# A hybrid layer on one core: the recurrence's output products of two blocks, moved from the end of the first phase into the projection of later blocks

## The chip, the cores and the metric

The kernel runs on one core of a Trainium2 chip. The metric is the device time of one execution in microseconds (us), here the median of three runs. The five engines are named as the profile names them: PE (TensorE, matrix products; PEld is its weight load), DVE (VectorE), ACT (ScalarE), POOL (GpSimd) and SP (SyncE, which here only issues DMAs). Each engine works through its own list of instructions in order. DMAs are issued from SP, ACT and POOL.

## The reference

One layer over a sequence of 2048 frames of width 1024, in float32. A projection feeds two mixers side by side: a delta-rule recurrence (RWKV-7, 8 heads of 64) and a differential attention (4 heads); their outputs share one output matrix, `w_out`. A cross attention to 256 memory tokens and a squared-ReLU MLP of width 4096 follow.

```
h = x
proj = rms_norm(h) @ w_in                       # 1792 columns recurrence, 1536 attention
y_rwkv = rwkv7_group(proj[:, :1792])            # sequential over frames, 512 wide
y_diff = diff_attn_group(proj[:, 1792:])        # block-causal, 512 wide
h = h + concat([y_rwkv, y_diff]) @ w_out
h = h + memory_cross_attn(rms_norm(h), rms_norm(mem))
h = h + square(relu(rms_norm(h) @ w_up)) @ w_down
out = rms_norm(h)
```

The rows 0 to 511 of `w_out` meet `y_rwkv`; the change is about this half of the product.

## The kernel before

Activations are held transposed, features on the 128 partitions and 512 frames (one of four blocks, numbered 0 to 3) on the free axis. Each large product is done in three matmuls per 128x128 weight tile, because both factors are split in a high and a low part (`whi`, `wlo` and, for activations, `xhi`/`xlo` or `yhi`/`ylo`): hi x hi, hi x lo, lo x hi. A weight half of 512 rows comes by one SP DMA of 256 KB into `wraw` (two buffers); ACT rounds it to `whi`, POOL subtracts for `wlo` (L612 to L616).

**The first phase** (`phase1`, L744) drives one stream of products, `inproj_stream` (L599), which yields after every three matmuls; three matmuls are a step. Its items are, in order: for each block the 26 column tiles of `w_in` (two lead tiles, 12 for the recurrence, 12 for the attention; 8 steps each), cut into eight segments; then seven attention tiles of block 3 held back (`late`); then the memory keys and values (`mem`, 16 items of 8 half-width steps), 8 products that fold `w_mo` into the values (`fold`), and the recurrence's output products (`wys`, 8 items of 4 steps for each of the four blocks). Of the latter, block 0's eight are interleaved with `mem` and `fold`; the 24 of blocks 1 to 3 come last (L840 to L844).

Around the stream runs the recurrence, in eight units (two per block, four heads each). `prep(u)` builds a unit's matrices and inverts them, `finish(u)` scans the 8 chunks and writes the result to a DRAM scratch, `s.yT` (L576). `run` (L911) sets how many stream steps are emitted between their pieces; both are wrapped in `urgent`, which gives their instructions a higher priority. The final order on each engine is written by the framework's planner, which takes priorities and a simulated timeline. The last two runs have `g.nd` = 170 steps beside `finish(6)` and `prep(7)`, and the rest beside `finish(7)` and `first_queries` (L941), the attention of block 0: four heads, two units each. Each such unit ends with L1136, which scales `ob`, and L1138, which stores it to `s.oT`.

An output product (`wy_items`, L711): before a block's first item, `pre` loads four slices of `s.yT` through `xsl` buffers (L723) and splits them into `yhi`/`ylo`, which take over the buffers of `xhi`/`xlo`. Each item loads the residual slice `xres` from `s.xT` on SP (L731) into a buffer of the tag `mix` (two buffers), runs 12 matmuls, adds on DVE (L738) and stores it back from ACT's queue (L739). The buffer is free when this store has landed.

`prep_x` (L232) fills `xhi`/`xlo` (one buffer each) at every block's start: eight slices, each a load into `xsl` (three buffers, L245), four transposes on PE (L247), a copy back into the same buffer on ACT (L249), a store to `s.xT` (L250), and the split. `x_stats` (L193) and `prep_mem` (L640) use the same three `xsl` buffers.

**The second phase** (`phase23`, L1471) first runs the rest of the layer for blocks 0 and 1 one after the other (`m_stream`, L1296), with the attention of blocks 1 to 3 (`d_stream`, L1142) interleaved, then blocks 2 and 3 together. `m_stream` for block 0 begins with `load_o` (L1287), which reads block 0's `s.oT` and splits it into `yh`/`yl` (L1221, L1222). The PSUM banks of the attention's scores in this phase are those that the first phase's `ps_acc` has used.

The 16 KiB per partition that the program builder sets aside for descriptors of POOL's DMAs is its default (L1544 gives no size). POOL issues in each unit a part of the transfers that carry the unit's matrices through DRAM (L418 to L468).

Of the kernel before, what the change touches and what calls it, by code (L numbers as in the profile page):

```python
# [16 lines left out]
P = 128  # L17
# [175 lines left out]
def x_stats(g, pool, blk):  # L193
    nc = g.nc
    ssx = g.small.tile([P, 2, 4], F32, tag="ssx", name="ssx")
    for j in range(4):
        for h in range(2):
            t = pool.tile([P, TB], F32, tag="xsl", name="xld", bufs=3)
            r0 = blk * TB + j * P
            nc.sync.dma_start(out=t, in_=g.i.x[0, r0:r0 + P, h * TB:(h + 1) * TB])  # L200
            nc.scalar.activation(out=t, in_=t, func=AF.Square, accum_out=ssx[:, h, j:j + 1])
    sst = g.small.tile([P, 4], F32, tag="sst", name="sst")
    nc.vector.tensor_tensor(out=sst, in0=ssx[:, 0, :], in1=ssx[:, 1, :], op=ALU.add)
    rstd = g.small.tile([P, 4], F32, tag="rstdx", name="rstdx")
    pow_rsqrt(g, rstd, sst, 4, 1.0 / D, RMS_EPS, "x")
    return rstd
# [25 lines left out]
def prep_x(g, pool, blk, rstd):  # L232
    nc = g.nc
    rows = slice(blk * TB, (blk + 1) * TB)
    psb = g.ps_acc.tile([P, TB], F32, tag="acc", name="psb")
    bcast_rows(g, psb, rstd, 4)
    sb = pool.tile([P, TB], F32, tag="sbx", name="sbx", bufs=1)
    nc.scalar.activation(out=sb, in_=psb, func=AF.Copy)
    out = []
    for k in range(KD):  # L240
        xt = pool.tile([P, 4, P], F32, tag="xsl", name="xsl", bufs=3)
        ps_pool, tag = (g.ps_misc, "misc") if blk == 0 and k % 2 else (g.ps_acc, "acc")
        ps = ps_pool.tile([P, TB], F32, tag=tag, name="ps_xt")
        if blk:
            nc.sync.dma_start(out=xt, in_=g.i.x[0, rows, k * P:(k + 1) * P].rearrange("(j p) c -> p j c", p=P))  # L245
        for j in range(4):
            nc.tensor.transpose(ps[:, j * P:(j + 1) * P], xt[:, j, :] if blk else g.xa[j][:, k * P:(k + 1) * P], g.ident)  # L247
        raw = xt.rearrange("p j c -> p (j c)")
        nc.scalar.activation(out=raw, in_=ps, func=AF.Copy)  # L249
        nc.sync.dma_start(out=g.s.xT[k * P:(k + 1) * P, rows], in_=raw)  # L250
        hi = pool.tile([P, TB], F32R, tag=f"xhi{k}", name="xhi", bufs=1)
        lo = pool.tile([P, TB], F32R, tag=f"xlo{k}", name="xlo", bufs=1)
        xn = pool.tile([P, TB], F32, tag="mix", name="xn", bufs=2)
        nc.vector.scalar_tensor_tensor(out=xn, in0=ps, scalar=g.col("nmix", k), in1=sb, op0=ALU.mult, op1=ALU.mult)
        nc.scalar.activation(out=hi, in_=xn, func=AF.Copy)
        eng = nc.gpsimd if blk == 0 and k % 2 else nc.vector
        eng.tensor_tensor(out=lo, in0=xn, in1=f32(hi), op=ALU.subtract)
        out.append((hi, lo))
    return out
# [380 lines left out]
def prep_mem(g, pool):  # L640
    nc = g.nc
    hs = [pool.tile([P, 2, MEMT], F32R, tag=f"xhi{k}", name="mh", bufs=1) for k in range(4)]
    ls = [pool.tile([P, 2, MEMT], F32R, tag=f"xlo{k}", name="ml", bufs=1) for k in range(4)]
    mh = lambda k: hs[k // 2][:, k % 2, :]
    ml = lambda k: ls[k // 2][:, k % 2, :]
    for j in range(2):
        ss = g.small.tile([P, 4], F32, tag="sst", name="ssm")
        ts_ = []
        for h in range(2):
            t = pool.tile([P, TB], F32, tag="xsl", name="mt", bufs=3)  # L650
            nc.sync.dma_start(out=t, in_=g.i.mem[0, j * P:(j + 1) * P, h * TB:(h + 1) * TB])
            junk = pool.tile([P, TB], F32, tag="mix", name="mj", bufs=2)
            nc.scalar.activation(out=junk, in_=t, func=AF.Square, accum_out=ss[:, h:h + 1])
            ts_.append(t)
        nc.vector.tensor_tensor(out=ss[:, 2:3], in0=ss[:, 0:1], in1=ss[:, 1:2], op=ALU.add)
        pow_rsqrt(g, ss[:, 3:4], ss[:, 2:3], 1, 1.0 / D, RMS_EPS, "x")
        for t in ts_:
            nc.vector.tensor_scalar(out=t, in0=t, scalar1=ss[:, 3:4], scalar2=None, op0=ALU.mult)
        ms = slice(j * P, (j + 1) * P)
        for k4 in range(2):  # L660
            ps = g.ps_acc.tile([P, 4, P], F32, tag="acc", name="ps_m")
            for k in range(4):
                nc.tensor.transpose(ps[:, k, :], ts_[k4][:, k * P:(k + 1) * P], g.ident)
            for k in range(4):
                kk = 4 * k4 + k
                w = g.col("nsrc", kk)
                nc.scalar.activation(out=mh(kk)[:, ms], in_=ps[:, k, :], func=AF.Copy, scale=w)
                nc.vector.scalar_tensor_tensor(out=ml(kk)[:, ms], in0=ps[:, k, :], scalar=w, in1=f32(mh(kk)[:, ms]),
                                               op0=ALU.mult, op1=ALU.subtract)
    return [(mh(k), ml(k)) for k in range(KD)]  # L670
# [37 lines left out]
    return kv, fold  # L708


def wy_items(g, pool, st, blk, key):  # L711
    nc = g.nc
    cs = slice(blk * TB, (blk + 1) * TB)
    xts = {}

    def pre(m):
        def f():
            if m == 0:
                ys = []
                for k in range(4):  # L720
                    kk = k + 4 * ((blk + 1) % 2)
                    raw = pool.tile([P, TB], F32, tag="xsl", name="yraw", bufs=3)
                    nc.sync.dma_start(out=raw, in_=g.s.yT[k * P:(k + 1) * P, cs])  # L723
                    hi = pool.tile([P, TB], F32R, tag=f"xhi{kk}", name="yhi", bufs=1)
                    lo = pool.tile([P, TB], F32R, tag=f"xlo{kk}", name="ylo", bufs=1)
                    nc.scalar.activation(out=hi, in_=raw, func=AF.Copy)
                    nc.vector.tensor_tensor(out=lo, in0=raw, in1=f32(hi), op=ALU.subtract)
                    ys.append((hi, lo))
                st[key] = [ys]
            xt = pool.tile([P, TB], F32, tag="mix", name="xres", bufs=2)  # L730
            nc.sync.dma_start(out=xt, in_=g.s.xT[m * P:(m + 1) * P, cs])  # L731
            xts[m] = xt
        return f

    def post(m):
        def f(ps):
            xt = xts[m]
            nc.vector.tensor_tensor(out=xt, in0=ps, in1=xt, op=ALU.add)  # L738
            nc.scalar.dma_start(out=g.s.xT[m * P:(m + 1) * P, cs], in_=xt)  # L739
        return f  # L740
    return [Item(key, g.i.w_out[0, :, m * P:(m + 1) * P], post(m), pre(m), TB, 1) for m in range(KD)]


def phase1(g, er):  # L744
# [3 lines left out]
    with ExitStack() as es:  # L748
# [81 lines left out]
        for b in range(1, NB):  # L830
            e = g.nlate if b == NB - 1 else 0
            segs.append(lead(b) + diffs(b, 0, 2) + rkv(2 * b) + diffs(b, 2, 3))
            a = min(2, 7 - e)
            segs.append(diffs(b, 5, a) + rkv(2 * b + 1) + diffs(b, 5 + a, 7 - e - a))
            if e:
                late = diffs(b, 12 - e, e)
        items = [it for sg in segs for it in sg] + late
        mem, fold = mem_items(g, pool, st, NB)
        wys = [it for b in range(NB) for it in wy_items(g, pool, st, b, NB + 1 + b)]
        for h in range(4):  # L840
            items += mem[2 * h:2 * h + 2] + wys[h:h + 1]
        for h in range(4):
# [68 lines left out]
        def run(gens, n):  # L911
            done = 0
            heads = [[next(x), i, x] for i, x in enumerate(gens)]
            while heads:
                h = min(heads)
                while done < h[0] * n:
                    next(stream, None)
                    done += 1
                t = next(h[2], None)
                if t is None:  # L920
                    heads.remove(h)
                else:
                    h[0] = t
            while done < n:
                next(stream, None)
                done += 1
        units = {}
        nst = [8 * len(sg) for sg in segs]
        rst[0] = x_first_stats(g, up)
        lora_load()  # L930
        run([], nst[0])
# [3 lines left out]
        run([urgent(g, finish(NU - 2), g.off_f), urgent(g, prep(NU - 1), g.off_p)], g.nd)  # L935
        el.close()
        dq = Ctx()
        run([urgent(g, finish(NU - 1, g.fin), g.off_f), urgent(g, first_queries(g, er, dq), g.off_q)], 8 * len(late) + 160 + 32 * NB - g.nd)


def first_queries(g, es, d):  # L941
# [15 lines left out]
def urgent(g, gen, offset):  # L957
    while True:
        with g.tc.high_priority(offset=offset):
            r = next(gen, None)  # L960
        if r is None and not isinstance(r, float) and gen.gi_frame is None:
            return
        yield r
# [592 lines left out]
```

## Time and profile before

| | |
|---|---|
| median of three runs | 3756.1 us (3751.57 to 3762.16) |
| profiled execution | 3768.81 us, its span 3767.1 us |
| PE busy | 3581.6 us, 95% of the span |
| DVE, ACT, POOL busy | 52%, 46%, 39% of the span |
| last projection matmul (L634) | starts at 1071.0 us |
| first use of `s.oT` by `m_stream` (L1221) | starts at 1422.1 us |

A busy PE counts the modelled length of a matmul from its start to its end, while the next one starts before that; so the distance from start to start tells what a matmul costs. Times are in us from the start of the span. The arrow in a row names what ended the idle time ahead of an instruction.

### The profile page before, as it was taken

To read this page: it belongs to the slowest core of one execution; us is meant where nothing else is said; L and a number is where in the kernel's file an instruction comes from. 1 tells how busy PE (TensorE), PEld (TensorE's weight loads), DVE (VectorE), ACT (ScalarE), POOL (GpSimd) and SP (SyncE) were. 2 spreads that over 40 slices of the span, in tenths; PEclk is the share of its full clock that TensorE was granted. 3 is DMA by queue.
4 is the path that set the end of the run, shared out by engine and by line. 5 is a ranking of instruction groups with operands and counts; after the bars stand their busy time and mean duration, and the time that the engine had idled before them with its cause. 6 is when DMAs were issued, how large, how long until landed. Compare 5 with 4: busy or idle time off the path is not lost. (4 is left out here: it accounts for less than half of the span.)

```text
span 3767.1 us, 57886 instructions
## 1 busy us (share of the span) xinstructions
PE 3581.6 (95%) x21297; PEld 2871.5 (76%) x21297; DVE 1957.9 (52%) x4093; ACT 1720.5 (46%) x3802; POOL 1464.5 (39%) x1195
## 2 busy tenths in 40 slices
PE   7999999999999878899999989999999999999998
PEld 5767766767777767678787777888878888888887
DVE  4456666666574636465566756666634332313132
ACT  5364464454455626554455765555543421212123
POOL 4424324423434534344435435343353332222225
PEclk9989999999999899999999999999999999999999
DMA  4343342333335674343324425232243331111113
GB/s 149 107 128 88 82 127 84 86 107 88 87 88 160 207 210 142 106 121 93 113 79 118 139 73 144 79 112 78 85 152 94 111 102 48 48 51 48 48 57 108
DMA packets 566066, 390.52 MB, mean 104 GB/s; under 512 B 65187, under 2 KB 491254, under 8 KB 565782
## 3 DMA queue, kind: packets, MB, share of 16 engines
q1 hardware_dynamic: 534134, 329.55, 30.5%
q10 hardware_dynamic: 28064, 50.35, 4.0%
q0 software_dynamic: 3584, 6.92, 0.8%
q8 instruction: 168, 2.75, 0.3%
q14 instruction: 116, 0.95, 0.1%
HBM read 311.14 MB, written 75.56 MB: 103 GB/s over the span
## 5 line engine op out<-in xcount | busy, mean ns | idle before, releaser
L170 POOL TENSOR_TENSOR wlo<-wraw,whi 128x512 fp32r<-128x512 f32 x520 | 689.5, 1327 | 1247.6 <-ACT whi L169 1218.6
L616 POOL TENSOR_TENSOR wlo<-wraw,whi 128x512 fp32r<-128x512 f32 x288 | 413.8, 1438 | 597.4 <-ACT whi L615 479.3
L169 ACT ACTIVATE whi<-wraw 128x512 fp32r<-128x512 f32 x520 | 327.9, 631 | 639.9 <-PE ps_dn L187 327.0
L186 PE MATMUL ps_dn<-hdh,whi 128*128 128x512 f32 x1024 | 402.1, 393 | 2.3 <-DVE t L1408 1.2
L187 PE MATMUL ps_dn<-hdl,whi 128*128 128x512 f32 x1024 | 401.8, 393 | 0.3 <-DVE hdl L1413 0.3
L188 PE MATMUL ps_dn<-hdh,wlo 128*128 128x512 f32 x1024 | 398.8, 393 | 3.3 <-POOL wlo L170 3.1
L186 PE MATMUL ps_up<-h2h,whi 128*128 128x512 f32 x1024 | 400.1, 391 | 1.0 <-DVE t L1408 0.9
L187 PE MATMUL ps_up<-h2l,whi 128*128 128x512 f32 x1024 | 400.7, 391 | 0.0
L188 PE MATMUL ps_up<-h2h,wlo 128*128 128x512 f32 x1024 | 395.3, 391 | 0.8 <-POOL wlo L170 0.8
L631 PE MATMUL ps_acc<-xhi,whi 128*128 128x512 f32 x832 | 343.7, 414 | 20.0 <-ACT carry L278 18.9
L634 PE MATMUL ps_acc<-xhi,wlo 128*128 128x512 f32 x832 | 343.8, 414 | 2.2 <-POOL wlo L616 2.0
L632 PE MATMUL ps_acc<-xlo,whi 128*128 128x512 f32 x832 | 340.3, 409 | 0.0
L615 ACT ACTIVATE whi<-wraw 128x512 fp32r<-128x512 f32 x288 | 181.2, 630 | 273.4 <-PE ps_acc L632 98.0
L1422 DVE TENSOR_TENSOR ht<-ht,ps_dn 128x512 f32<-128x512 f32 x128 | 87.8, 686 | 347.3 <-PE ps_dn L188 347.2
L1048 ACT ACTIVATE pt<-ps_s,nmx 128x512 f32<-128x512 f32 (+3 forms) x320 | 198.4, 621 | 142.4 <-DVE nmx L1047 117.9
L1047 DVE TENSOR_REDUCE nmx<-ps_s 128x1 f32<-128x512 f32 (+3 forms) x320 | 192.5, 606 | 75.6 <-PE ps_s L1044 71.6
L188 PEld LDWEIGHTS ps_dn<-hdh,wlo 128*128 128x128 f32 x1024 | 193.1, 189 | 45.3 <-POOL wlo L170 6.4
L186 PEld LDWEIGHTS ps_dn<-hdh,whi 128*128 128x128 f32 x1024 | 193.0, 188 | 41.8 <-issue 1.6
L186 PEld LDWEIGHTS ps_up<-h2h,whi 128*128 128x128 f32 x1024 | 192.1, 188 | 41.3 <-DVE t L1408 1.6
L187 PEld LDWEIGHTS ps_dn<-hdl,whi 128*128 128x128 f32 x1024 | 193.2, 189 | 39.8 <-DVE hdl L1413 0.5
L188 PEld LDWEIGHTS ps_up<-h2h,wlo 128*128 128x128 f32 x1024 | 192.4, 188 | 40.3 <-POOL wlo L170 1.5
L187 PEld LDWEIGHTS ps_up<-h2l,whi 128*128 128x128 f32 x1024 | 192.3, 188 | 38.8
(336 smaller groups left out, 7772.4 us busy)
## 6 DMA issues: line engine op xcount, KB each, us to landing
wraw<-in_w_in_dram SPq DMA_DIRECT2D x208, 256.0 KB
wraw<-in_w_down_dram SPq DMA_DIRECT2D x208, 256.0 KB
wraw<-in_w_up_dram SPq DMA_DIRECT2D x192, 256.0 KB
s_hT<-xt ACTq DMA_DIRECT2D x64, 256.0 KB
wraw<-in_w_out_dram SPq DMA_DIRECT2D x56, 256.0 KB
s_qkvT<-qkv ACTq DMA_DIRECT2D x48, 256.0 KB
wraw<-in_w_mq_dram SPq DMA_DIRECT2D x48, 256.0 KB
wraw<-s_mb SPq DMA_DIRECT2D x48, 256.0 KB
```

The costliest lines, as they stand in the source:

```text
L169: nc.scalar.activation(out=hi, in_=raw, func=AF.Copy)
L170: nc.gpsimd.tensor_tensor(out=lo, in0=raw, in1=f32(hi), op=ALU.subtract)
L186: nc.tensor.matmul(ps, whi(k), ahi(k), start=(k == 0), stop=False)
L187: nc.tensor.matmul(ps, whi(k), alo(k), start=False, stop=False)
L188: nc.tensor.matmul(ps, wlo(k), ahi(k), start=False, stop=(k == nk - 1))
L615: nc.scalar.activation(out=hi, in_=raw, func=AF.Copy)
L616: nc.gpsimd.tensor_tensor(out=lo, in0=raw, in1=f32(hi), op=ALU.subtract)
L631: nc.tensor.matmul(o, hi[:, kk, :], xs[k][0], start=(k == 0), stop=False)
L632: nc.tensor.matmul(o, hi[:, kk, :], xs[k][1], start=False, stop=False)
L634: nc.tensor.matmul(o, lo[:, kk, :], xs[k][0], start=False, stop=last)
L1047: nc.vector.tensor_reduce(out=nmx[:, m, c:c + 1], in_=ps[:, 0:w], axis=AX.X, op=ALU.max, negate=True)
L1048: nc.scalar.activation(out=pt[:, cw(c)], in_=ps[:, 0:w], func=AF.Exp, bias=nmx[:, m, c:c + 1], accum_out=sm[:, m, c:c + 1])
```

## The change

The eight output products of block 0 are put into the fifth and sixth segment (the projection of block 2), those of block 1 into the seventh and eighth (block 3). Each segment takes four, the first ahead of the segment's third last item, the others between the following items and after the last. They get tiles of their own, `yh0` to `yh3` and `yl0` to `yl3`, 16 KiB per partition. That space comes from `xsl`, which goes from three buffers to two in all its uses (2 KiB), and from the space for POOL's descriptors, which goes from the default to 2048 bytes (14 KiB). At the end of the phase block 2's eight products take the places that block 0's had, and block 3's eight come last. The count of steps follows: a segment's steps are now summed from its items, and the last run has 64 steps fewer.

```diff
-        xt = pool.tile([P, 4, P], F32, tag="xsl", name="xsl", bufs=3)
+        xt = pool.tile([P, 4, P], F32, tag="xsl", name="xsl", bufs=2)
...
-def wy_items(g, pool, st, blk, key):
+def wy_items(g, pool, st, blk, key, own=False):
...
-                    hi = pool.tile([P, TB], F32R, tag=f"xhi{kk}", name="yhi", bufs=1)
-                    lo = pool.tile([P, TB], F32R, tag=f"xlo{kk}", name="ylo", bufs=1)
+                    th, tl = (f"yh{k}", f"yl{k}") if own else (f"xhi{kk}", f"xlo{kk}")
+                    hi = pool.tile([P, TB], F32R, tag=th, name="yhi", bufs=1)
+                    lo = pool.tile([P, TB], F32R, tag=tl, name="ylo", bufs=1)
...
+        for b in range(NB - 2):
+            early = wy_items(g, pool, st, b, NB + 1 + b, True)
+            for j in range(2):
+                sg = segs[2 * b + 4 + j]
+                at = len(sg) - 3
+                for i, w in enumerate(early[4 * j:4 * j + 4]):
+                    sg.insert(min(at + 2 * i, len(sg)), w)
         items = [it for sg in segs for it in sg] + late
         mem, fold = mem_items(g, pool, st, NB)
-        wys = [it for b in range(NB) for it in wy_items(g, pool, st, b, NB + 1 + b)]
+        wys = [it for b in range(NB - 2, NB) for it in wy_items(g, pool, st, b, NB + 1 + b)]
...
-        nst = [8 * len(sg) for sg in segs]
+        nst = [sum(4 * it.nh for it in sg) for sg in segs]
...
-        run([urgent(g, finish(NU - 1, g.fin), g.off_f), urgent(g, first_queries(g, er, dq), g.off_q)], 8 * len(late) + 160 + 32 * NB - g.nd)
+        run([urgent(g, finish(NU - 1, g.fin), g.off_f), urgent(g, first_queries(g, er, dq), g.off_q)], 8 * len(late) + 160 + 64 - g.nd)
...
-    nc = _bacc.Bacc("TRN2", target_bir_lowering=False, num_devices=1)
+    nc = _bacc.Bacc("TRN2", target_bir_lowering=False, num_devices=1, dynamic_dma_scratch_size=2048)
```

The other lines of the diff set `bufs=2` for `xsl` in `x_stats`, `prep_mem` and `wy_items`.

## Rows read from the trace of the kernel before

**Rows 1.** Windows: stretch, length, busy PE, PEld, DVE, ACT, POOL, clock, DMA share, GB/s.
```profile
1312.00:1424.00 112.00, 86.89 (x367) 68.11 (x365) 37.56 (x87) 30.72 (x67) 37.30 (x31) 0.92 0.70 203
...
300.00:1071.00 771.00, 742.05 (x6413) 542.50 (x6412) 485.40 (x1225) 376.77 (x917) 283.34 (x251) 0.96 0.34 94
```

**Rows 2.** Waits of all engines, 1240 to 1430: total us, times, longest.
```profile
DVE xres L738 <- DMA xres<-s_xT: 45.9, 16, 6.4
PE ps_acc L631 <- DVE xres L738: 19.1, 11, 4.2
```

**Rows 3.** Waits of SP's queue, 1240 to 1430.
```profile
SPq L731 <- DMA s_xT<-xres: 56.0, 17, 6.5
```

**Rows 4.** Timeline of PE, end of the projection: start, us, instruction.
```profile
1069.16 0.40 PE L631 MATMUL ps_acc<-xhi,whi 128*128 128x512 f32 x1
...
1071.00 0.39 PE L634 MATMUL ps_acc<-xhi,wlo 128*128 128x512 f32 x1
```

**Rows 5.** Waits of PE, 300 to 1070.
```profile
PE ps_acc L631 <- ACT carry L278: 13.8, 9, 2.1
...
PE ps_xt L247 <- DMA xsl<-in_x_dram: 3.2, 1, 3.2
```

**Rows 6.** Waits of PE, 1071 to 1240.
```profile
PE ps_acc L631 <- DVE xres L738: 1.3, 1, 1.3
```

**Rows 7.** Timeline of DVE, first and last addition of the trailing 24 products.
```profile
1319.87 0.69 DVE L738 TENSOR_TENSOR xres<-ps_acc,xres 128x512 f32<-128x512 f32 x1 [5.71 <-DMA xres<-s_xT]
...
1418.36 0.69 DVE L738 TENSOR_TENSOR xres<-ps_acc,xres 128x512 f32<-128x512 f32 x1 [2.11 <-DMA xres<-s_xT]
```

**Rows 8.** Timeline of DVE, ends of three units of the first phase's attention.
```profile
1290.41 0.40 DVE L1136 SCALAR_TENSOR_TENSOR ob<-ob,d_sub,psb 128x256 f32<-128x256 f32 x1
...
1310.87 0.47 DVE L1136 SCALAR_TENSOR_TENSOR ob<-ob,d_sub,psb 128x256 f32<-128x256 f32 x1
...
1397.44 0.47 DVE L1136 SCALAR_TENSOR_TENSOR ob<-ob,d_sub,psb 128x256 f32<-128x256 f32 x1
```

**Rows 9.** Timeline of PE and ACT where the second phase begins.
```profile
1419.11 0.80 PE L1043 MATMUL ps_s<-ks,qa 128*128 128x512 f32 x1 [3.64 <-DVE xres L738]
...
1421.09 0.69 ACT L1048 ACTIVATE pt<-ps_s,nmx 128x512 f32<-128x512 f32 x1 [17.41 <-DMA s_xT<-xres]
...
1422.12 1.14 ACT L1221 ACTIVATE yh<-yraw 128x512 fp32r<-128x512 f32 x2
```

**Rows 10.** Line 985, 1200 to 1423: count, ns min/median/max, first and last start.
```profile
L985 ACT ACTIVATE ks<-draw x10: 615/632/634, 1225.2 to 1312.5; 128x512 fp32r<-128x512 f32 x10
```

**Rows 11.** Timelines of PE, SP and DVE while block 3's slices are prepared.
```profile
796.35 0.66 PE L247 MATMUL ps_xt<-ident,xsl 128*128 128x128 f32 x4
...
798.40 0.34 SPq L250 DMA_DIRECT2D s_xT<-xsl  x1
...
802.21 0.37 SPq L245 DMA_DIRECT2D xsl<-in_x_dram  x1
...
819.23 0.38 SPq L245 DMA_DIRECT2D xsl<-in_x_dram  x1
...
824.21 0.66 PE L247 MATMUL ps_xt<-ident,xsl 128*128 128x128 f32 x4 [3.22 <-DMA xsl<-in_x_dram]
...
829.32 0.68 DVE L257 TENSOR_TENSOR xlo<-xn,xhi 128x512 fp32r<-128x512 f32 x1
```

**Rows 12.** Windows of 10 us while block 1's slices are prepared.
```profile
220.00:230.00 10.00, 7.24 (x55) 4.70 (x55) 9.71 (x20) 5.87 (x15) 2.58 (x1) 0.89 0.44 142
230.00:240.00 10.00, 10.00 (x61) 8.18 (x61) 9.78 (x18) 7.02 (x18) 0.00 (x0) 0.50 0.42 131
240.00:250.00 10.00, 10.00 (x58) 7.97 (x58) 9.06 (x17) 5.25 (x14) 0.70 (x1) 0.50 0.50 156
```

**Rows 13.** POOL's DMA issues of one kind, whole run (count, busy, mean ns, idle before).
```profile
L468 POOL DMA_DIRECT2D NTs<-LT x16 | 9.3, 588 | 8.0 <-DMA LT<-X 8.0
```

**Rows 14.** Waits of POOL, 700 to 1180.
```profile
POOL NTs L468 <- DMA LT<-X: 5.0, 3, 3.3
```

More of the change, by code (lines that the diff above doesn't have):

```diff
@@ L197, in x_stats @@
         for h in range(2):
-            t = pool.tile([P, TB], F32, tag="xsl", name="xld", bufs=3)
+            t = pool.tile([P, TB], F32, tag="xsl", name="xld", bufs=2)
             r0 = blk * TB + j * P
@@ L649, in prep_mem @@
         for h in range(2):
-            t = pool.tile([P, TB], F32, tag="xsl", name="mt", bufs=3)
+            t = pool.tile([P, TB], F32, tag="xsl", name="mt", bufs=2)
             nc.sync.dma_start(out=t, in_=g.i.mem[0, j * P:(j + 1) * P, h * TB:(h + 1) * TB])
@@ L721, in f @@
                     kk = k + 4 * ((blk + 1) % 2)
-                    raw = pool.tile([P, TB], F32, tag="xsl", name="yraw", bufs=3)
+                    raw = pool.tile([P, TB], F32, tag="xsl", name="yraw", bufs=2)
                     nc.sync.dma_start(out=raw, in_=g.s.yT[k * P:(k + 1) * P, cs])
-                    hi = pool.tile([P, TB], F32R, tag=f"xhi{kk}", name="yhi", bufs=1)
-                    lo = pool.tile([P, TB], F32R, tag=f"xlo{kk}", name="ylo", bufs=1)
+                    th, tl = (f"yh{k}", f"yl{k}") if own else (f"xhi{kk}", f"xlo{kk}")
+                    hi = pool.tile([P, TB], F32R, tag=th, name="yhi", bufs=1)
+                    lo = pool.tile([P, TB], F32R, tag=tl, name="ylo", bufs=1)
                     nc.scalar.activation(out=hi, in_=raw, func=AF.Copy)
```

## The prediction

> **What bounds the kernel now.** I read the windows first, to see where PE has room. Over the projection, 300 to 1071 us, PE is busy 742 of 771 us; over the end of the first phase, 1312 to 1424, it is busy 86.9 of 112, with the DMA engines at a share of 0.70 against 0.34 in the projection [rows 1]. So the projection is PE's own, and the end is not: 25.1 us of it are idle.
>
> The waits say who holds the end. DVE's addition of the residual (L738) waits 45.9 us for the load of `xres`, and PE waits 19.1 us for that addition, because the product cannot start before one of its two PSUM buffers is free [rows 2]. SP's queue in turn waits 56.0 us, before it may issue the load of `xres`, for the landing of an earlier store of the same buffer [rows 3]. That is a loop of load, add, store over two `mix` buffers, and each product has to go through it. When such products lie between items of another kind (block 0's eight, 1100 to 1240), the same wait of PE is 1.3 us [rows 6]. The loop only binds when products follow each other.
>
> **What a product costs in each place.** Two matmuls of the projection start 1069.16 and 1071.00, eight intervals apart: 0.23 us each [rows 4]. A product of 12 costs PE 12 x 0.23 = 2.76 us where PE is the bound. In the trailing run of 24, the first addition starts at 1319.87 and the last at 1418.36: 98.5 / 23 = 4.28 us a product [rows 7].
>
> **The change, part by part**, against the profiled execution (3768.8 us, 12.7 above the median; I carry the difference over to the median).
>
> 1. Sixteen products into the projection. PE is the bound there: + 16 x 2.76 = + 44.2 us. With each product come a weight load, a conversion on ACT, a subtraction on POOL, one residual load and one store; these engines and the DMAs have the room of [rows 1] (POOL 283 of 771 us, ACT 377). Each product lies between projection items of 24 matmuls, 5.5 us, in which its buffer's store can land; [rows 6] is the nearest row for that, so I take no wait. If the cover failed, each would cost the 4.28 of the end: 16 x 1.52 = 24 us more.
> 2. Idle time that they fill. PE waits 13.8 us in the projection for an item's last copy on ACT (L278), with both PSUM buffers held [rows 5]. A product between two such items gives the copy 2.76 us more. Only some of the sixteen stand there (in the eighth segment, beside recurrence tiles): between 0 and 13.8, and I take - 4.
> 3. Two `xsl` buffers instead of three. From block 3's preparation I take one buffer's round: load 824.21 - 819.23 = 5.0, transposes 0.66, the copy on ACT about as long, and the store's landing 802.21 - 798.40 = 3.8; some 10.1 us [rows 11]. Over two buffers that is 5.05 us a slice, 40 us for eight; over three it took 829.32 + 0.68 - 796.35 = 33.7. So each of three boundaries gets some 7 us longer. PE has the recurrence to do meanwhile: with three buffers it waited 3.2 us for such a load in all of 300 to 1070 [rows 5]. Bounds 0 and 3 x 7 = 21 us; I take the lower part, + 6, since the row nearest shows PE nearly covered. A gain is excluded: nothing starts earlier for a buffer less.
> 4. Less space for POOL's descriptors. The rows show its issues short (0.59 us for the smaller gather [rows 13]) and waiting only for data. No row shows an issue that waits for space. I take 0; the other end is rival D.
> 5. Sixteen products out of the trailing run: - 16 x 4.28 = - 68.5 us, if nothing else becomes late.
> 6. What is late next: the attention of block 0 (`first_queries`). Its fifth unit ends at 1310.87, its eighth at 1397.44; those three had to queue behind DVE's and PE's waits for residuals, at 28.9 us each, while the fifth came 20.5 us after the fourth [rows 8]. `m_stream` needs the last one: its first conversion starts at 1422.12, and 17.4 of these 24.7 us ACT was held by a residual store [rows 9]. Without the trailing products I put the three units at 20.5 each and the handover at 24.7 - 17.4 = 7.3: 68.8 us after 1310.87 instead of 111.3, so `m_stream` starts 42.4 us earlier, not 68.5. In the gap of 26.1 us PE has two chains: `first_queries`, and the attention of blocks 1 to 3, whose first scores started at 1419.11 as soon as the last residual was added and PSUM came free [rows 9]; ten key conversions had been done by 1312.5, of which four are already its own, since the three later heads of block 0 need six [rows 10]. The three units took 86.9 - 24 x 2.76 = 20.7 us of PE [rows 1], in 61.5 us a share of 0.34; two chains 0.68. So 0.32 x 26.1 = + 8.4 us stay idle (bounds 0 and 26.1).
>
> Sum: + 44.2 - 4 + 6 + 0 - 68.5 + 8.4 = - 13.9 us, 3768.8 to 3754.9 on the profiled scale, **3742 us** on the scale of the median.
>
> **The rivals.**
>
> A, the forecast, has bounds of its own: without items 3 and the gap - 28.3 (3728), with a gap half idle and 9 us at the boundaries - 6 (3750).
>
> B: block 0's attention sets the end and nothing fills the gap. Then the end gives back 42.4, not 60: 44.2 - 4 + 6 - 42.4 = + 3.8, 3760; with 21 us at the boundaries 3775. For it: a unit is a chain over four engines that less PE work shortens little, and `m_stream` cannot start without it. Against it: the scores that were ready at 1419.
>
> C, slower: the two-buffer staging starves PE at the block boundaries. Its place is the three runs of `prep_x`. [...] Against it: at the boundaries of blocks 2 and 3 the wait was 3.2 us in all [rows 5], and at the last one a product that needs no `xhi` now closes the segment before.
>
> D: POOL's issues wait for descriptor space. If the four gathers that close an inverse went out one landing at a time, at the longest wait for a landing seen on POOL, 3.3 us [rows 14], a unit would come 3 x 3.3 = 10 us later. In the projection PE has other work; two units at the end have less: + 20, 3762; with all eight exposed + 80, 3822.
> [...] No run here shows at what size an issue would wait.
>
> That the products are not run where they are put is unlikely: they hold a place in one stream whose items share PSUM in turn.
>
> **How the numbers follow.** A 0.52, B 0.27, C 0.13, D 0.08. The measurement can tell about 0.3%, 11 us, from no change. Faster than 3745: most of A (0.40) and a little of B (0.03), 0.43. Within 11 us: the rest of A (0.12), most of B (0.22), some of D (0.03), 0.37. Slower: C, some of D and of B, 0.20. The range goes from 3716 (A's lower end, and 12 us in which the planner, with the end of the phase cleared, starts the second phase's attention still earlier) to 3774 (B with the boundaries at their bound); C and the far part of D lie outside. A alone: 3728 to 3750.
>
> **What would show it.** After the change, the last projection matmul (1071.0 [rows 4]) should start some 46 us later, near 1117; the distance between matmuls there stays 0.23. PE's wait for residual additions at the end of the phase should fall from 19.1 to under 8 us. The last `ob` should come within 65 us of the fifth, and the first `yh` conversion within 12 us of the last `ob`; scores of block 1 should start before it. If instead the projection's end moves by 60 us or more, with waits for `xsl` loads or clock slices at 0.50 at the boundaries, it was C; if POOL sits idle ahead of its DMA issues, D; if PE idles more than 15 us between the last product and the first `yh`, B. The forecast is wrong in its root if the sixteen products cost the 4.28 us in their new place too.

## The result and the profile after

The changed kernel takes 3781.2 us (median of four runs, 3778.3 to 3785.7) against 3753.9 (four runs of the kernel before beside it): a ratio of 1.0063, interval 1.0047 to 1.0080. By the ratio it is 24 us slower; 14 us faster was forecast. Its profiled execution took 3781.1 us, span 3779.4. In the sessions of the experiments, on four chips, the kernel before took 3762.8 to 3767.2 us (medians of 17 to 28 runs), and the changed kernel was not run there; so the size of the loss is less certain than its interval says.

What did come as forecast first. The DVE timeline of the kernel after (start, duration, the instruction) answers to [rows 7, 8]: the additions of the trailing run and two units of block 0's attention, the fifth and the last.

```profile
1383.16 0.47 DVE L1144 SCALAR_TENSOR_TENSOR ob<-ob,d_sub,psb 128x256 f32<-128x256 f32 x1
...
1409.21 0.69 DVE L739 TENSOR_TENSOR xres<-ps_acc,xres 128x512 f32<-128x512 f32 x1 [3.56 <-DMA xres<-s_xT]
...
1436.86 0.69 DVE L739 TENSOR_TENSOR xres<-ps_acc,xres 128x512 f32<-128x512 f32 x1 [4.13 <-DMA xres<-s_xT]
1440.85 0.48 DVE L1144 SCALAR_TENSOR_TENSOR ob<-ob,d_sub,psb 128x256 f32<-128x256 f32 x1 [0.71 <-PE psb L158]
```

The trailing run has eight products, at (1436.86 - 1409.21) / 7 = 3.95 us. From the fifth `ob` to the last it is 57.7 us (86.6 before), and the handover is short, as the first conversion of `m_stream` on ACT's timeline shows, 5.4 us after the last `ob` (24.7 before [rows 8, 9]):

```profile
1446.22 0.63 ACT L1229 ACTIVATE yh<-yraw 128x512 fp32r<-128x512 f32 x1 [0.48 <-issue]
```

PE's waits from 1240 to 1450 (total, times, longest) show that residual additions hold PE for the 3.4 us of this row and 0.5 us elsewhere, against 19.1 us [rows 2];

```profile
PE ps_s L1051 <- DVE xres L739: 3.4, 1, 3.4
```

and SP's queue waits for the stores of `xres` in the same stretch no longer than this, against 56.0 us [rows 3]:

```profile
SPq L732 <- DMA s_xT<-xres: 16.3, 4, 6.5
```

So the end of the phase is what was forecast in kind. But `m_stream` starts at 1446.2 instead of 1422.1, 24 us later. (The two profiled executions differ by only 12.3 us in the end, spans 3779.4 and 3767.1, because the second phase took 2333 us against 2345. That the 24 us here equal the 24 by the ratio is therefore partly luck.) The projection is still PE's, busy 835 of 873 us, as the window to its end shows (length, then PE busy), against 742 of 771 in [rows 1]:

```profile
300.00:1173.00 873.00, 835.39 (x6968) 609.40 (x6967) 540.61 (x1348) 409.62 (x995) 313.11 (x277) 0.96 0.36 102
```

Its last matmul, on PE's timeline, comes 102 us later than in [rows 4], not 46, at the same distance of 0.23 us:

```profile
1172.99 0.40 PE L632 MATMUL ps_acc<-xlo,whi 128*128 128x512 f32 x1
1173.22 0.40 PE L634 MATMUL ps_acc<-xhi,wlo 128*128 128x512 f32 x1
```

**Where the time went.** I split the first phase where the recurrence's last matrices are done (the last `A<-psw` of unit 7: 1183 before, 1250 after); from there on the last scan, block 0's attention and the rest of the stream run to the first `yh`. The windows (length, then PE busy and its instructions, PEld, DVE, ACT, POOL, granted clock) of the kernel before:

```profile
0.00:1183.00 1183.00, 1115.01 (x9199) 824.58 (x9200) 706.27 (x1776) 577.01 (x1381) 448.17 (x419) 0.95 0.37 104
1183.00:1422.00 239.00, 202.53 (x1176) 161.99 (x1175) 111.41 (x290) 116.29 (x278) 104.18 (x83) 0.92 0.67 199
```

and of the kernel after:

```profile
0.00:1250.00 1250.00, 1159.98 (x9327) 852.35 (x9327) 724.29 (x1799) 585.19 (x1396) 454.37 (x427) 0.94 0.37 107
1250.00:1446.00 196.00, 167.29 (x1062) 134.89 (x1058) 103.84 (x272) 107.04 (x270) 94.86 (x76) 0.93 0.60 180
```

PE issues the same work in both (10375 and 10389 matmuls to `yh`) and is busy 92 to 93% of the phase, so a product moved inside it can win little but idle time. The front grew by 67 us, the end shrank by 43. In the front PE's idle time (length less busy) rose from 68.0 to 90.0 us; in the end it fell only from 36.5 to 28.7. Idle time is thus 14 of the 24 us; for the other 10 PE was busy longer with nearly the same matmuls.

**The block boundaries.** The windows of the three units in which a block's slices are prepared (units 1, 3 and 5 of 0 to 7), before:

```profile
208.00:348.00 140.00, 136.18 (x1140) 99.52 (x1139) 93.67 (x236) 76.32 (x188) 49.42 (x43) 0.90 0.39 113
488.00:624.00 136.00, 129.51 (x1125) 94.75 (x1125) 94.94 (x232) 74.30 (x183) 48.94 (x42) 0.92 0.41 117
765.00:902.00 137.00, 129.58 (x1150) 96.40 (x1150) 94.28 (x230) 70.47 (x170) 46.73 (x43) 0.96 0.38 106
```

and after, with unit 4 (141 us before) between the last two:

```profile
211.00:360.00 149.00, 140.71 (x1135) 100.23 (x1134) 95.30 (x235) 76.17 (x189) 46.78 (x42) 0.89 0.37 107
496.00:650.00 154.00, 143.41 (x1150) 105.37 (x1148) 97.11 (x238) 79.52 (x193) 49.66 (x45) 0.90 0.41 116
650.00:800.00 150.00, 146.75 (x1184) 106.19 (x1180) 85.87 (x217) 64.92 (x158) 55.88 (x48) 0.97 0.32 91
800.00:958.00 158.00, 148.20 (x1215) 110.09 (x1212) 101.66 (x240) 76.55 (x181) 53.30 (x47) 0.91 0.43 122
```

The three take 9, 18 and 21 us longer: 48 of the front's 67 (some of it work: units 3 and 5 hold more matmuls, 25 and 65). But not all of this belongs to the buffer. In `after_x3` (below), which has three `xsl` buffers again, units 1, 3, 4 and 5 are:

```profile
207.00:355.00 148.00, 142.69 (x1141) 104.84 (x1141) 93.64 (x236) 76.73 (x190) 49.52 (x44) 0.86 0.39 109
488.00:628.00 140.00, 131.81 (x1138) 96.83 (x1138) 99.37 (x238) 78.73 (x192) 47.93 (x44) 0.94 0.45 125
628.00:765.00 137.00, 135.20 (x1158) 97.33 (x1157) 84.67 (x217) 63.66 (x157) 53.25 (x47) 0.99 0.34 94
765.00:928.00 163.00, 147.15 (x1210) 107.94 (x1209) 100.13 (x238) 77.96 (x181) 51.95 (x49) 0.95 0.43 120
```

The third buffer gives back 14 us in unit 3 and 13 in unit 4, and nothing in units 1 and 5. Unit 5 goes with the moved products: it takes 158 to 166 us in every kernel below with block 0's products early and three buffers, and 135 to 140 in those without. Unit 1 takes 148 us in `alias_only` too, which moves no product and has three buffers.

In ten-microsecond slices of unit 3, the kernel after, the granted clock is at the lower of its two levels for a whole slice and part of the next, after a slice in which PE was busy 8.64 of 10 us:

```profile
520.00:530.00 10.00, 8.64 (x80) 6.92 (x79) 9.77 (x17) 7.22 (x20) 1.33 (x1) 0.89 0.59 157
530.00:540.00 10.00, 9.35 (x56) 6.13 (x54) 6.63 (x13) 4.14 (x12) 1.25 (x2) 0.50 0.47 134
540.00:550.00 10.00, 10.00 (x81) 6.12 (x81) 5.61 (x11) 6.45 (x17) 1.78 (x3) 0.76 0.27 87
```

The kernel before has such a slice in this unit as well, so the clock does not tell the two apart here (for block 1 see [rows 12]):

```profile
520.00:530.00 10.00, 10.00 (x65) 6.75 (x63) 8.19 (x16) 5.65 (x16) 1.26 (x2) 0.59 0.56 160
```

PE's own waits from 300 to 1173, which answer to [rows 5] (13.8 and 3.2), name the slices for only 6.9 us (5.4 in `after_x3`):

```profile
PE ps_acc L631 <- ACT carry L278: 11.8, 10, 2.2
PE ps_xt L247 <- DMA xsl<-in_x_dram: 6.9, 6, 2.2
```

### The profile page after: what moved, and what is told of

It reads as the page before. It is cut to its first block, busy times and chain, and to the rows that moved or that the text cites. A ratio compares the mean times of both kernels' runs of the same rounds, so it can differ in the third digit from the quotient of the medians.

```text
span 3779.4 us, 57866 instructions
## 1 busy us (share of the span) xinstructions
PE 3589.3 (95%) x21297; PEld 2870.4 (76%) x21297; DVE 1969.6 (52%) x4093; ACT 1716.5 (45%) x3802; POOL 1459.9 (39%) x1195
```

## The experiments

Two executions with the same instruction order on every engine (the kernel before and `scratch_only`, below) differ by 21.6 us, and by 20 us already at the first `yh`. The ends of their fronts lie 18 us apart, 1183 and 1165, with PE idle for 68.0 and 62.5 us in them. So verdicts go by the ratios of many runs, one hundredth of which is 38 us; a single marker of a trace is good to some 20 us. The sessions ran on different chips, so a comparison of two ratios from different sessions also rests on the kernel before behaving alike on both. Also, the planner writes a new order for every edit; I take it, without a run that shows it, that kernels can differ by some 10 us for this alone.

**x2_only.** The kernel before with `xsl` alone cut:

```diff
-tag="xsl", ..., bufs=3
+tag="xsl", ..., bufs=2
```

> Before, with two xsl buffers instead of three and nothing else. Staging theory (the shorter buffer chain at the three block boundaries is the loss): 10 to 30 us slower than before, with the units that hold a boundary (about 208 to 348, 488 to 624, 765 to 902 us) each 5 to 15 us longer and the others unchanged. Displacement theory (the sixteen products cost the projection more than their 44 us of PE, or the end gives back too little): within 5 us of before. Descriptor theory (POOL waits for space): within 5 us of before.

Measured: 1.0030 (1.0013 to 1.0047), + 11 us (5 to 18). PE's idle time in the front rises from 68.0 to 80.8:

```profile
0.00:1195.00 1195.00, 1114.17 (x9199) 817.66 (x9200) 712.89 (x1776) 578.20 (x1382) 446.48 (x419) 0.95 0.36 103
```

The two buffers alone cost 11 us without a product moved; the 6 that I took lies just inside the interval. The sign that was to go with it came at one boundary of three: units 1, 3 and 5 take 149, 134 and 137 us.

**scratch_only.** The kernel before with the smaller descriptor space:

```diff
-num_devices=1)
+num_devices=1, dynamic_dma_scratch_size=2048)
```

> Before, with 2048 bytes for POOL's descriptors and nothing else; every engine's instructions stay in the same order. Descriptor theory: 10 us slower or more, with longer idle time ahead of or inside POOL's DMA issues (the smaller gather took 0.59 us). Staging and displacement theory: within 4 us of before.

Measured: 0.9992 (0.9980 to 1.0003). Rival D falls.

**after_x3.** The change with three `xsl` buffers; the room comes from writing the inverse's `T` into the buffer of `N`:

```diff
-tag="xsl", ..., bufs=2
+tag="xsl", ..., bufs=3
-        u.T = lp.tile([P, NCK, CH], F32, tag="T", name="T", bufs=2)
+        u.T = TT[:, p]        # TT = lp.tile([P, 2, NCK, CH], F32, tag="N", ...)
```

> After, with three xsl buffers again; the 2 KiB come from the inverse's pool, where the merged matrices T take over the buffer of N, which is dead by then. Staging theory: the boundary units fall back by some 10 us each, 20 to 40 us faster than after, so 0 to 15 us faster than before. Displacement theory: like after, some 25 us slower than before.

Measured: 0.9997 (0.9982 to 1.0013): the loss is gone, and so is any gain. Against the change itself, 1.0063, the third buffer is worth 0.66%, 25 us (16 to 34). The two ratios come from different sessions; the plain medians, 3781.2 and 3771.1, are 10 us apart. The front ends at 1220 instead of 1250:

```profile
0.00:1220.00 1220.00, 1141.11 (x9283) 841.90 (x9283) 720.73 (x1798) 583.04 (x1389) 448.02 (x425) 0.95 0.39 109
1220.00:1425.00 205.00, 172.62 (x1096) 139.60 (x1094) 100.15 (x271) 107.52 (x272) 96.47 (x78) 0.91 0.61 180
```

**alias_only**, its control: the kernel before with that `T` in `N` and the small descriptor space.

> A control: the kernel before with the smaller descriptor space and the transform T written into the buffer of N, as in after_x3 and the kernels made from it; no product is moved and xsl keeps three buffers. If that edit is harmless, as the comparisons with after_x3, only0 and only1 assume, the ratio is 0.998 to 1.002, the projection ends within 6 us of 1071 and block 0's last inverse within 8 us of 1183. If the edit itself delays or speeds a unit (T can be written only when N's last readers are done, and the next N only when T's are), the ends of the units drift from 208, 348, 488, 624, 765, 902, 1044, 1183 by a constant amount per unit, and the ratio leaves 0.998 to 1.002; the gain of only0 (0.9923) is then partly the alias.

Measured: 1.0012 (0.9998 to 1.0025), inside the bound for harmless; in its trace, whose time was 10 us above its median, unit 7 ended at 1194, past the 8 us allowed. If the sharing costs anything, it is some 5 us (9 at most by the interval), and it makes the kernels that carry it look worse, not better.

**only0** and **only1.** after_x3 with the eight products of only one block early:

```diff
-        for b in range(NB - 2):
+        for b in [0]:        # only1: [1]
```

> As after with three xsl buffers, but only block 0's eight products are early (fifth and sixth segment); block 1's go back to the end of the phase. Alignment theory (the early products of block 0 push block 3's slice preparation, at 796 to 830 us before, into the inverse of the seventh unit, where PE has no recurrence work and the stream has to wait for xhi): preparation at 850 us or later, the unit that ends at 902 us in before lasts 20 us or more longer than its 137 us, and the kernel is 0 to 12 us slower than before. Chain theory (the end of the phase is set by block 0's attention, which takes some 200 us from the end of the last inverse, so every product ahead of that inverse is lost time): 0 to 10 us slower for the same eight products, but with no special loss at block 3's boundary.

> As after with three xsl buffers, but only block 1's eight products are early (seventh and eighth segment). Alignment theory: no boundary is pushed, block 3's preparation stays at 796 to 830 us, and the kernel is 5 to 20 us faster than before, and faster than only0 by 10 us or more. Chain theory: the same as only0 within 8 us, because the same eight products lie ahead of the last inverse.

Measured: only0 0.9923 (0.9904 to 0.9942), 29 us faster than before, the best of all that do the whole work; only1 0.9969 (0.9957 to 0.9981). The first eight gain 29 us, and the second eight, put beside them, lose them again, though alone they gain 12. Neither theory of the expectations had this: both put only0 at no gain or a loss, and only1 level with it or ahead. One sign of the alignment theory came: in only0 block 3's slices are loaded until 863 us (819 before), and the unit that holds this takes 159 us. The windows of only0:

```profile
0.00:1199.00 1199.00, 1129.07 (x9314) 835.03 (x9315) 714.74 (x1788) 582.39 (x1395) 455.76 (x427) 0.95 0.39 109
1199.00:1395.00 196.00, 168.19 (x1069) 135.73 (x1068) 101.76 (x282) 107.46 (x268) 94.11 (x76) 0.95 0.67 200
```

Its end is as short, 196 us, as that of the kernel after with twice the products moved; after_x3's is 205. From eight products to sixteen the front pays another 21 us, and the end gives nothing more. (In only1 the front ends at 1178 and the end is 233 us long, both within 6 us of the kernel before.) The second phase took 2334 us in only0 and 2344 in after_x3; why, no row here tells.

**only0_x2.** only0 with two `xsl` buffers (and without the shared `T`).

> After exactly as changed, two xsl buffers included, but only block 0's eight products are early. Staging theory: it loses against only0 what two buffers cost with early products (25 us between after and after_x3) or without (11 us): 11 to 25 us slower than only0, so 4 to 18 us faster than before. If two buffers cost only through the second block's loads: within 8 us of only0.

Measured: 1.0046 (1.0027 to 1.0066). Beside only0 the two buffers cost 1.23%, 46 us (36 to 56), four times what they cost the kernel before, and more than the 11 to 25 expected. What the products have to do with `xsl` is on SP's queue in the kernel after, in the preparation of block 2 and behind it (start, duration of the issue):

```profile
526.13 1.91 SPq L245 DMA_DIRECT2D xsl<-in_x_dram  x2
...
534.31 2.75 SPq L245 DMA_DIRECT2D xsl<-in_x_dram  x2
...
544.82 0.37 SPq L245 DMA_DIRECT2D xsl<-in_x_dram  x1
...
562.87 6.54 SPq L200 DMA_DIRECT2D xld<-in_x_dram  x4
570.81 0.33 SPq L200 DMA_DIRECT2D xld<-in_x_dram  x1
572.77 0.33 SPq L723 DMA_DIRECT2D yraw<-s_yT  x1
574.91 0.33 SPq L723 DMA_DIRECT2D yraw<-s_yT  x1
577.92 0.94 SPq L723 DMA_DIRECT2D yraw<-s_yT  x1
582.49 0.46 SPq L723 DMA_DIRECT2D yraw<-s_yT  x1
```

Two slices come every 8 to 10 us, so 4 to 5 us each; then the eight `xld` of the next block's statistics and the four `yraw` of the moved products go through the same two buffers, one by one. In only0, with three, the four `yraw` have been issued by 556.82 (of the 26 us between the two, the kernel after was 15 behind when the unit began, at 496 against 481):

```profile
547.45 4.21 SPq L724 DMA_DIRECT2D yraw<-s_yT  x3
556.82 0.32 SPq L724 DMA_DIRECT2D yraw<-s_yT  x1
```

That the `yraw` loads are what multiplies the cost is read from these rows and not tried by itself. Their number alone does not give it: the change, with twice as many, pays 25 us for the buffer, only0_x2 46.

**at_boundary.** after_x3, with block 0's eight products as a group at the end of the sixth segment, and block 1's behind `late`:

```diff
-            for j in range(2):
-                ...
-                    sg.insert(min(at + 2 * i, len(sg)), w)
+            (segs[5], late)[b].extend(early)
```

> As after with three xsl buffers, but block 0's eight products stand together behind the sixth segment's last item, where the stream waits for block 3's slices, and block 1's eight behind the late tiles, where it waits for the memory tokens' slices. Alignment theory: PE's idle time at these two places (some 25 us in the kernel with products among the last three items) is filled, the kernel is 10 to 25 us faster than before. Chain theory: they still stand ahead of the last inverse; what they fill is gained, the rest is not: 5 us faster to 5 us slower than before.

Measured: 0.9980 (0.9965 to 0.9996), 8 us faster than before, between the two theories, and 6 us from after_x3, which is within the noise of the two. The place decides less than the number (after_x3 and only0 are 28 us apart).

**light16.** after_x3 with a third of the matmuls of the sixteen:

```diff
+            if not it.light:
                 nc.tensor.matmul(o, hi[:, kk, :], xs[k][1], start=False, stop=False)
                 nc.tensor.matmul(o, lo[:, kk, :], xs[k][0], start=False, stop=last)
```

> The changed kernel with three xsl buffers (after_x3), in which the sixteen early products run only the first of the three partial products of each weight tile: 4 matmuls instead of 12, so the low parts of these sixteen products are left out. Loads, conversions, additions, stores, PSUM turns and places are as they were. In after_x3 the projection ends 84 us later than before (1155 against 1071), 5.2 us a product. If these 84 us are TensorE's time, taken from a stream that has only the share of TensorE which the recurrence leaves (2.76 us of matmuls cost 4.9 to 5.2), a third of the matmuls costs a third: the projection ends near 1071 + 28 = 1099, and the kernel takes 40 to 55 us less than after_x3 (0.985 to 0.990 of the kernel before). If they are what stands around the matmuls (a PSUM turn, weight halves through two buffers, the residual's load and store, the shift of block 3's preparation into the sixth unit's inverse), the projection still ends at 1130 or later, and the kernel stays within 20 us of after_x3 (0.994 to 1.001).

Measured: 0.9924 (0.9906 to 0.9942); the projection ends at 1109. This is between the two theories. 128 matmuls fewer, 29.4 us at 0.23, make the kernel 0.73%, 27.5 us (18 to 37), faster than after_x3: in the kernel as a whole a matmul costs 0.14 to 0.29 us, which holds the plain 0.23 and needs no multiplier, and little of the moved work is covered. Loads, conversions, additions and PSUM turns stay in light16, so it doesn't price them. That the projection's end moved by more (46 us) says only that the stream is the one that yields when the recurrence runs ahead of it. The windows show the other half: the last residual addition is at 1372.44, and from there to the first `yh` at 1400 PE idles 7.3 of 28 us.

```profile
1372.00:1400.00 28.00, 20.69 (x87) 15.42 (x88) 21.93 (x70) 19.55 (x57) 5.20 (x5) 0.74 0.32 101
```

Block 0's last `ob` comes at 1392.26 there, 20 us after every product is done: the end is 192 us long and no longer waits for products.

**noatt_before, noatt_after_x3, noatt_only0.** The kernel before, after_x3 and only0 without block 0's attention in the first phase, to see whether it is the floor of the end:

```diff
-    for i, _ in enumerate(d_stream(g, d, 1, [0])):
-        yield g.fq * i / n
+    ...                      # per head and half: memset ob to 0.5, store it to s.oT, yield
```

> Before, with block 0's attention in the first phase left out (its output is filled with a constant, so the result lacks that attention). Floor theory (from the end of the last inverse, block 0's attention takes some 195 to 215 us, and the second phase's first conversion cannot come sooner): before was held by its trailing products, not by the floor, so it gains only the attention's own PE work and waits, 25 to 60 us. Loop theory alone (no floor, only the residual buffers and PE): the same.

> After with three xsl buffers, and block 0's attention left out in the same way. Floor theory: after_x3 stood at the floor (last attention output at 1418, last product at 1419), so without it the end falls to the products alone: at least 15 us faster than noatt_before, and within 8 us of noatt_only0, where the pair with attention differs by 27 us. If there is no floor: noatt_after_x3 and noatt_only0 stay 20 to 30 us apart, and noatt_after_x3 is within 8 us of noatt_before, as with attention.

> Only block 0's eight products early, three xsl buffers, block 0's attention left out in the same way. Floor theory: it already stood at the floor with its products (both ended at 1388), so it gains less than noatt_after_x3 does against after_x3; the two end within 8 us. No floor: 20 to 30 us faster than noatt_after_x3.

Measured: 0.9933 (0.9911 to 0.9954), 0.9929 (0.9904 to 0.9953), 0.9914 (0.9896 to 0.9933). Without the attention the sixteen products bring nothing either. The floor theory said that noatt_after_x3 would gain 15 us on noatt_before, and falls as the only cause. Its other sign came, against the theory without a floor: noatt_after_x3 and noatt_only0 are 6 us apart, where with the attention it is 28. So most of only0's gain, too, is there only with the attention in place (noatt_only0 is 7 us ahead of noatt_before, within the noise). From noatt_before to noatt_after_x3 (windows in this order) the end becomes 37 us shorter, and the front 44 longer.

```profile
1178.00:1393.00 215.00, 171.76 (x949) 128.40 (x949) 56.42 (x106) 78.33 (x169) 86.37 (x67) 0.93 0.65 198
```

```profile
1222.00:1400.00 178.00, 142.68 (x897) 110.39 (x894) 41.26 (x78) 70.96 (x158) 81.23 (x63) 0.92 0.60 181
```

**mix4** and **mix4_xsl5.** The kernel before, no product moved, with the small descriptor space spent on buffers: four `mix` instead of two; then five `xsl` as well.

```diff
-tag="mix", ..., bufs=2
+tag="mix", ..., bufs=4
```

> Before, with four mix buffers instead of two (the space comes from the descriptors' 14 KiB); no product is moved. If the load-add-store loop over two buffers sets the pace of the trailing 24 products: their additions come closer than 4.28 us, near 3 us, PE's wait for residuals falls from 19 us to under 5, and the kernel is 10 to 30 us faster. If block 0's attention sets the end whatever the products do (rival B of the prediction): the products speed up and the end moves by less than 8 us.

> Before, with four mix buffers and five xsl buffers, from the descriptors' space; no product is moved. Staging theory: the boundaries with three xsl buffers still cost something, so 3 to 12 us faster than four mix buffers alone (which was 21 us faster than before). If three buffers already cover the boundaries (the wait for such loads was 3.2 us in all): the same as four mix buffers alone, within 4 us.

Measured: 0.9944 (0.9920 to 0.9968) and 0.9969 (0.9957 to 0.9982). With the loop of [rows 2, 3] loosened, DVE waits for products, and hardly for the load of `xres` (its waits from 1290 to 1400, against 45.9 us in [rows 2]):

```profile
DVE xres L738 <- PE ps_acc L634: 20.1, 8, 7.8
...
DVE xres L738 <- DMA s_xT<-xres: 3.6, 1, 3.6
DVE xres L738 <- DMA xres<-s_xT: 2.8, 1, 2.8
```

Some 70% of only0's gain (21 of 29 us, with intervals that overlap) is to be had by buffers alone. The trailing additions come every (1394.05 - 1304.01) / 23 = 3.91 us, not near 3 as expected, and the end is 13 us shorter (226); the front is 12 us shorter too, where `mix` also serves the projection's copies, so the gain isn't shown to be the residual loop's alone. Why two `xsl` more take 10 us off that, I cannot say; the two intervals overlap.

## Why the prediction was wrong, step by step

The bound was read rightly (PE in the projection, the residual loop at the end). Two terms of the sum were mis-sized, the third buffer (step 3) and the end (steps 5 and 6); the others held or are not shown to have failed:

1. Sixteen products, + 44.2: the matmuls' price held. light16 gives 27.5 / 128 = 0.215 us a matmul against 0.23. Whether a whole product costs as much as 4.28 in the new place, the "root", is not settled: light16 leaves the rest of a product in place, and the ratio of after_x3 gives only the difference between the cost in front and the gain at the end.
2. Idle time filled, - 4: the wait for `carry` fell from 13.8 to 11.8, in after_x3 to 6.6; within its bounds.
3. **Two `xsl` buffers, + 6: failed.** 25 us in the change (after against after_x3), 11 alone, 46 beside block 0's products. The 25 lies above the bound of 21, which is inside its interval (16 to 34). I had the slice's round right (4 to 5 us a slice over two buffers, the traces show), and took PE's short wait for a load as proof that PE is covered. It is not how the loss shows: PE's wait for slices is 6.9 us with two buffers and 5.4 with three, while units 3 and 4 take 27 us longer with two. Of these 27 PE's idle time is 4; 38 more matmuls (8.7 us at 0.23) fall into them, and what lengthens them otherwise stays open. And the edit gave `xsl` new customers, the eight `yraw` of the moved products, that the step didn't count.
4. Descriptor space, 0: held.
5. and 6. **The end, - 68.5 + 8.4 = - 60.1: 43 us came.** The markers came true (57.7 us under 65, 5.4 under 12, PE's wait 3.9 under 8), so this is a matter of size. PE's busy time in the end fell by 35.2 us, not 44: the projection had slipped behind the recurrence, and more of the stream now ran after unit 7's matrices. And its idle time fell by 7.8, not by the 15.9 that 60.1 less 44.2 implies. The size is that of rival B, 42.4.

By the ratios alone the two misses are of like size: the third buffer cost 19 us more than I took, and with it in place (after_x3) the rest of the sum, - 19.9, came to - 1 (- 7 to + 5). The traces say the same: front 44.2 - 4 + 25 = 65 (67 in the trace), end - 43, together + 22 where 24 was measured. That this closes to 2 us is luck: the end of the front alone is good to 18 us, and the 12 us by which the second phase was shorter in that trace are not in the sum.

So the result has rival C's place, the boundaries, and B's size at the end, but neither rival's mechanism is shown. By the text's own test it was C (the projection's end moved over 60 us, slices at 0.50 at the boundaries). That test does not separate: after_x3, with its three buffers, moves the projection's end by 84 us and has a slice at 0.57, and the kernel before has such slices too. B was to show as PE idle for over 15 us between the last product and the first `yh`. In the kernel after only 9 us lie between the last addition and the first `yh`, and in light16 PE idles 7.3 of 28 us.

What of the end stays open: why it gives back no more than some 40 us. Block 0's attention ends last where products are out of the way (light16, 192 us), but without the attention sixteen moved products still bring nothing. There ACT's longest waits in the end are for weight loads, as those of noatt_after_x3 from 1222 to 1400 show, 52.5 us of 178; I have not separated these from the planner's order.

```profile
ACT whi L616 <- DMA wraw<-in_w_mv_dram: 18.1, 10, 4.3
ACT whi L616 <- DMA wraw<-in_w_out_dram: 17.6, 10, 3.6
ACT whi L616 <- DMA wraw<-in_w_mo_dram: 16.8, 10, 2.9
```

## What to carry to other kernels

Where an engine is busy for 93% of a stage, count a move inside it by idle time: what leaves the slack end arrives at near its full price in front, and the end gave back no more here for sixteen products than for eight. When room is made by taking a buffer from a shared tag, list every user of that tag after the edit, the moved work's own loads included, and price it by a run with that one buffer changed: a short wait on the bounding engine is no proof of cover. Here 6.9 us of waits stood beside a buffer worth some 25. And before moving work out of a run that a buffer loop slows, try the buffers.

## What the runs showed of the hardware

The same order of instructions took 136 us for unit 3 in one execution and 131 in another, with a granted clock of 0.92 and 0.99; here is the row of `scratch_only` beside that of before above:

```profile
482.00:613.00 131.00, 123.91 (x1129) 90.78 (x1127) 94.46 (x232) 74.94 (x185) 48.58 (x42) 0.99 0.44 123
```

Runs of one kernel spread over 28 us (3750.7 to 3778.7 in 28 runs of the kernel before on one chip). Their granted clocks lie between 0.966 and 0.973, and the longer runs tend to have the lower one (correlation - 0.60); how much of the spread the clock makes is not shown. And an eighth of the default descriptor space, 2048 bytes, cost POOL's DMAs nothing that the ratio shows (0.9992).
